# A hybrid SSD, GLA, cross-attention and SwiGLU block on one core: the Strassen-Winograd sums of three weights made by accumulating DRAM transfers instead of GpSimd

## The chip, the cores and the metric
The kernel runs on one core of a Trainium2 chip, as one launch. The metric is the device time of one execution, in microseconds (us), as the median of several runs. Five engines work beside one another, each through its own queue, in order: PE (TensorE: matmuls, with PEld, its weight loads), DVE (VectorE), ACT (ScalarE), POOL (GpSimd) and SP (SyncE, which here only issues DMAs). 16 DMA engines move the data of all queues.

## The reference, cut to what matters
One decoder block over a sequence of 1024 rows with D = 1024: an SSD branch and a GLA branch on one projection `w_in`, merged through gates, then cross-attention to 256 rows of memory, then SwiGLU with d_ff = 2816. All in float32. The three products that the change touches are those with `w_o`, `w_xq` and `w_ffn_out`:

```python
    merged = jax.nn.sigmoid(g_ssd) * (y_ssd @ w_up_ssd) + jax.nn.sigmoid(g_gla) * (y_gla @ w_up_gla)
    return merged @ w_o
    ...
    q = (n @ w_xq).reshape(Bsz, S, XATTN_HEADS, XATTN_HEAD_DIM)
    ...
    g, u = jnp.split(n @ w_ffn_in, 2, axis=-1)
    return (jax.nn.silu(g) * u) @ w_ffn_out
    ...
        h = h + hybrid_mixer(rmsnorm(h, norm_mix[i]), ...)
        h = h + mem_cross_attention(rmsnorm(h, norm_xattn[i]), ...)
        h = h + swiglu(rmsnorm(h, norm_ffn[i]), w_ffn_in[i], w_ffn_out[i])
    return rmsnorm(h, norm_final)
```

## The kernel before
**Products.** Every operand in float32 is split into a high part (`hi`, a rounding copy on ACT) and a low part (`lo`, a subtraction on DVE), and each product is three matmuls of 128x512: hi x lo, hi x hi, lo x hi. Where it pays, a product is a Strassen-Winograd product over 2x2 blocks: seven block products named `B11`, `B21`, `B22`, `T1` to `T4` in place of eight. Each needs sums of blocks of the weight (S1 to S4) and of the activations, and after it the results are added up (`evac` and `fevac`). `T1h`/`T1l` are the split halves of an activation sum, `whi`/`wlo` those of a streamed weight, `ws` those of w_o and w_xq, `fs` those of w_ffn_out.

**Stages, in us from the span's start.** Keys, values and the input up to 160; the units of z (160 to 240) and of xBC with the convolution (240 to 390), each a 1 MB load `raw` of w_in; the remaining units with SSD and GLA woven in to 800; the two up-projections, dense, to 980; w_o (class `Wide`) to 1040 and w_xq to 1100; attention to 1205; w_xo, dense, to 1281; the first SwiGLU product to 1705, in 11 pairs of a gate unit and an up unit, 38.8 us a pair; the down-projection to 1905; the closing norm to 1940. In a unit the sums of the weight are made on the fly from `raw`: `sa<-raw`, `sa<-sa,raw`, `raw<-raw` and `raw<-raw,sa`, on POOL or DVE. A helper `either` takes the engine that by a running count (`Meter`, a time per instruction and element) is free first. In such counts the calls on POOL are included, DMAs too.

**The sums of the three other weights.** They don't fit that pattern, since `Wide` and the down-projection load S1 to S4 from DRAM (`wos_d`, `xqs_d`, `down_d`). `presum(part, key)` (from line 1401) writes them. Per block of 128 rows it loads the four quadrants (1 MB) from the weight, makes the sums with four TENSOR_TENSORs on POOL (one addition and three subtractions) and stores each with an SP DMA of 256 KB. 8 blocks are of w_o and w_xq, 11 of w_ffn_out: 19 blocks, 76 sums. It runs in three parts: `early` (blocks 0 to 7, w_o and w_xq) in the up-projections, 800 to 980 us, with the buffer `pre` in a slot of the pool "m"; `late` (blocks 8 to 12) in attention and w_xo, with `pre` in a slot of the pool "op"; `last_sums` (blocks 13 to 18) in SwiGLU, over four `ga` tiles. The slots of "op" are handed on: when `late` ends, the slot that `pre` had is used by the split `B21l` of SwiGLU's activations, whose residual rows are `o` and `ga`. Around line 1700 the loop over w_xo takes two steps of `late` for each product.

**Order.** A tile scheduler orders the instructions by data dependences and priorities; `pinned` keeps an instruction at the place where it is written. `run(main, (side, rate))` draws `rate` steps of a side generator for each step of the main one. Each queue then runs in that order.

## Time and profile before
| | us |
|---|---|
| median of 3 runs | 1945.46 (1941.2 to 1947.19) |
| profiled execution | 1941.48 |
| its span | 1939.8 |
| PE busy | 1900.3 (98%) |
| DVE busy | 1391.4 (72%) |
| ACT busy | 879.8 (45%) |
| POOL busy | 611.7 (32%) |
| mean granted clock of TensorE | 0.995 of full speed |

The span is the time from the first to the last instruction of the profiled execution. A share of busy time is a mean over stages with different limits; which wait ends last in a stage tells what a change there can be worth. The rows below are in the form of the profile: start, duration, engine, line, operation, out<-in, and in brackets the idle time before the instruction with what ended it.

### The profile page before, as it was taken

How to read it: one execution, taken by the hardware profiler on the slowest of the kernel's cores; microseconds unless marked ns; L12 is line 12 of the kernel's file. 1: busy time of each engine (PE TensorE's matmuls, PEld its weight loads, DVE VectorE, ACT ScalarE, POOL GpSimd, SP SyncE). 2: the span in 40 equal slices, each digit the busy share in tenths (PEclk: the TensorE clock that was granted, in tenths of full speed). 3: DMA queues.
4: the chain of work that ended last, by engine and by line, in shares of the span. 5: the costliest groups of instructions: out<-in, count | busy, mean ns of one | idle time of the engine just before them, and what ended most of it. 6: DMA issues, size and time to landing. Idle time of an engine off the chain costs nothing.

```text
span 1939.8 us, 26274 instructions
## 1 busy us (share of the span) xinstructions
PE 1900.3 (98%) x9680; PEld 1599.7 (82%) x9680; DVE 1391.4 (72%) x1926; ACT 879.8 (45%) x1521; POOL 611.7 (32%) x455
## 2 busy tenths in 40 slices
...
GB/s 343 144 94 102 131 300 115 147 163 183 184 161 121 208 169 125 330 356 273 229 174 202 177 66 47 261 137 114 137 163 152 130 150 150 50 298 246 156 222 124
DMA packets 245365, 341.06 MB, mean 176 GB/s; under 512 B 17370, under 2 KB 148676, under 8 KB 245236
## 3 DMA queue, kind: packets, MB, share of 16 engines
q1 hardware_dynamic: 243508, 333.09, 50.7%
...
## 4 chain that ended last, share of the span: by engine, by line
PE 76%; DVE 9%; DMA 7%; POOL 3%; issue 3%; ACT 2%; SPq 0%; POOLq 0%; DVEq 0%; ACTq 0%
PE acc L51 60%; PE bank L51 14%; DVE cv L73 2%; POOL pre L73 2%; DVE wlo L73 2%; PE bank L55 2%; DMA pre<-in_w_xq_dram 1%; DMA pre<-in_w_ffn_out_dram 1%; DVE o L73 1%; DMA zr<-sz_d 1%; DVE hs L73 1%; POOL sa L73 1%; DMA down_d<-pre 1%; DMA xqs_d<-pre 1%; DMA wr<-wos_d 0%
## 5 line engine op out<-in xcount | busy, mean ns | idle before, releaser
L73 DVE TENSOR_TENSOR wlo<-raw,whi 128x512 fp32r<-128x512 f32 x272 | 245.8, 912 | 96.8 <-ACT whi L229 94.6
L229 ACT ACTIVATE whi<-raw 128x512 fp32r<-128x512 f32 x272 | 169.4, 628 | 237.4 <-PE acc L51 191.3
L51 PE MATMUL acc<-hl,wd 128*128 128x512 f32 x1152 | 263.8, 390 | 1.7 <-ACT wd L229 1.3
L51 PEld LDWEIGHTS acc<-hl,wd 128*128 128x128 f32 x1152 | 215.5, 188 | 48.3 <-ACT wd L229 2.5
L73 DVE TENSOR_TENSOR o<-acc,o 128x512 f32<-128x512 f32 (+1 forms) x256 | 172.3, 674 | 86.9 <-PE acc L51 77.4
L51 PE MATMUL acc<-fs 128*128 128x512 f32 (+1 forms) x792 | 155.7, 355 | 0.1
L51 PEld LDWEIGHTS acc<-fs 128*128 128x128 f32 x792 | 130.7, 189 | 20.8 <-issue 0.5
L73 DVE TENSOR_TENSOR fs<-fr,fs 128x1024 fp32r<-128x1024 f32 (+1 forms) x84 | 98.9, 1217 | 37.5 <-ACT fs L229 37.4
L229 ACT ACTIVATE fs<-fr 128x1024 fp32r<-128x1024 f32 (+1 forms) x84 | 79.0, 982 | 96.0 <-PE acc L51 30.7
L73 POOL TENSOR_TENSOR raw<-raw,sa 128x512 f32<-128x512 f32 x44 | 57.4, 1305 | 202.3 <-DVE wlo L73 202.3
L73 POOL TENSOR_TENSOR sa<-pre 128x512 f32<-128x512 f32 x13 | 19.3, 1485 | 290.0 <-DMA pre<-in_w_o_dram 103.1
L229 ACT ACTIVATE whi<-sa 128x512 fp32r<-128x512 f32 x96 | 59.6, 626 | 94.8 <-PE acc L51 89.2
L73 POOL TENSOR_TENSOR sa<-raw 128x512 f32<-128x512 f32 x43 | 68.4, 1590 | 106.5 <-DMA raw<-in_w_in_dram 77.0
L73 DVE TENSOR_TENSOR wlo<-sa,whi 128x512 fp32r<-128x512 f32 x96 | 82.2, 856 | 14.2 <-ACT whi L229 13.3
L51 PE MATMUL acc<-ws 128*128 128x512 f32 x384 | 89.1, 390 | 1.7 <-DVE ws L73 1.7
L51 PEld LDWEIGHTS acc<-ws 128*128 128x128 f32 x384 | 71.8, 188 | 17.2 <-DVE ws L73 2.2
L51 PE MATMUL acc<-B11h,whi 128*128 128x512 f32 x192 | 75.9, 395 | 2.5 <-ACT whi L229 2.5
L51 PE MATMUL acc<-T4h,whi 128*128 128x512 f32 x192 | 76.2, 397 | 2.0 <-DVE o L73 2.0
L51 PE MATMUL acc<-T1h,wlo 128*128 128x512 f32 x192 | 76.0, 396 | 1.7 <-DVE wlo L73 1.7
L51 PE MATMUL acc<-B11h,wlo 128*128 128x512 f32 x192 | 76.0, 396 | 1.5 <-DVE wlo L73 1.5
L51 PE MATMUL acc<-B22h,wlo 128*128 128x512 f32 x192 | 75.8, 395 | 1.5 <-DVE wlo L73 1.4
L51 PE MATMUL acc<-T1h,whi 128*128 128x512 f32 x192 | 77.2, 402 | 0.0
...
## 6 DMA issues: line engine op xcount, KB each, us to landing
raw<-in_w_in_dram SPq DMA_DIRECT2D x26, 1024.0 KB, 5.9
raw<-in_w_ffn_in_dram SPq DMA_DIRECT2D x22, 1024.0 KB, 9.3
...
fr<-act_d SPq DMA_DIRECT2D x35, 512.0 KB, 6.1
fr<-down_d SPq DMA_DIRECT2D x20, 512.0 KB, 4.7
...
csb<-cs_d SPq DMA_DIRECT2D x15, 512.0 KB, 4.4
fr<-in_w_ffn_out_dram SPq DMA_DIRECT2D x15, 512.0 KB, 3.8
```

Source lines behind the costliest of these rows:

```text
L51: return s.e.matmul(o, x, y, **kw)
L55: return s.e.transpose(o, x, i)
L73: return f(*a, **kw)
L229: ACT.activation(hi, src, AF.Copy)
```

## The change
`presum` and its three parts are gone. In place of them `weight_sums` makes the four sums with DMAs from DRAM to DRAM, issued on POOL's queue: a plain copy of a quadrant of the weight into the place of a sum, or a transfer that adds to what lies there (`accum_op=ALU.add`). For w_o and w_xq it runs in the units of z and xBC (`wsums`, rate 0.36; 24 DMAs: per weight four copies of 1 MB and four accumulations, each cut in two of 0.5 MB), for w_ffn_out in the pairs of SwiGLU (`last_sums`, groups of 3, 3, 3 and 2 blocks; 32 DMAs of 0.75 or 0.5 MB). Nothing is summed from 390 us to SwiGLU. An accumulating transfer can only add, so the second block row of the weight is taken with the other sign: all four sums then are sums with plus. The signs are made good elsewhere: by operands in the other order in the sums of the activations, by a split with `neg` (scale -1 in ACT's copy, SCALAR_TENSOR_TENSOR for the low half) for the right operand of `T2`, and by sub for add, or a scale of -1, in the evacuations.

```diff
+    def split(src, hi, lo, e=None, neg=False, pin=lambda x: x):
+        if neg:
+            pin(ACT.activation(hi, src, AF.Copy, scale=-1.0))
+            pin(DVE.scalar_tensor_tensor(lo, src, -1.0, hi, ALU.mult, ALU.subtract))
...
+    def weight_sums(todo):
+        jobs = []
+        for A, d, n, k0 in todo:
+            put = lambda m, d=d, n=n, k0=k0, kn=A.shape[2]: (
+                d[(m * n + k0) * P:(m * n + k0 + kn) * P].rearrange("(k p) c -> p k c", p=P))
+            q = {(i, j): A[j][:, :, half(i)] for i in range(2) for j in range(2)}
+            jobs.append([(put(0), q[1, 0], 0), (put(2), q[0, 0], 0), (put(3), q[0, 1], 0), (put(0), q[1, 1], 1),
+                         (put(2), q[1, 0], 1), (put(1), put(0), 0), (put(1), q[0, 0], 1), (put(3), put(1), 1)])
+        for step in zip(*jobs):
+            for o, a, more in step:
+                kn = o.shape[1]
+                for c in (slice(0, kn // 2), slice(kn // 2, kn)) if more and kn > 3 else (slice(0, kn),):
+                    if more:
+                        pinned(POOL.dma_start(o[:, c], a[:, c], accum_op=ALU.add))
+                    else:
+                        pinned(POOL.dma_start(o, a))
+                    yield
...
-    run(singles(zu, B, xu[:1]), (prep, 1.0))
+    run(singles(zu, B, xu[:1]), (prep, 1.0), (wsums, 0.36))
...
+    drain(wsums)
...
-                    DVE.scalar_tensor_tensor(o, p, s.scale, o, ALU.mult, ALU.add)
+                    DVE.scalar_tensor_tensor(o, p, -s.scale if i else s.scale, o, ALU.mult, ALU.add)
                 elif first:
-                    ACT.activation(o, p, AF.Copy)
+                    ACT.activation(o, p, AF.Copy, scale=-1.0 if i else 1.0)
+                elif name == "T3":
+                    sub(DVE, o, o, p)
...
-    early = presum(slice(0, 8), "m")
...
-    late = presum(slice(8, 13), "op")
...
-    last_sums = presum(slice(13, None), "ga")
+    w_down = t["w_ffn_out"].rearrange("(k j p) c -> j p k c", j=2, p=P)
+    last_sums = chain(weight_sums([(w_down[:, :, k:min(k + 3, KP)], down_d, KP, k)]) for k in range(0, KP, 3))
...
-        run(group([gate], B, () if last else gu[u + 1][:1]), (last_sums, 0.33))
+        run(group([gate], B, () if last else gu[u + 1][:1]), (last_sums, 0.4))
...
-            if n in (2, 5):
+            if n == 2:
                 next(last_sums, None)
```

The instructions of the changed program: PE 9171 matmuls as before and in nearly the same order, ACT 1465 as before, DVE 1947 for 1924 (10 more `raw<-raw,sa`, 10 more `o<-o,ssum`, 3 others), POOL 417 for 460 (76 sums gone, 23 moved to DVE, 56 DMAs come), SP 687 for 800.

**POOL in the units of z.** `raw` is the weight unit, `sa` its sums; the numbers tell buffers apart. Before:

```order
L73 TENSOR_TENSOR raw_1941<-raw_1941,sa_1988 128x4x128 [waits DVE_49,Pool_49]
L73 MEMSET keep_2053 128x1 [waits Pool_49]
L73 MEMSET keep_2053 128x1 x7
L73 TENSOR_TENSOR sa_2200<-raw_2170 128x512 [waits DMAHW0_49]
L73 TENSOR_TENSOR sa_2202<-sa_2200,raw_2170 128x512 [waits Pool_49]
L73 TENSOR_TENSOR raw_2170<-raw_2170 128x4x128
L73 TENSOR_TENSOR raw_2170<-raw_2170,sa_2202 128x4x128 [waits DVE_49,Pool_49]
L73 TENSOR_TENSOR sa_2354<-raw_2326 128x512 [waits DMAHW1_49]
L73 TENSOR_TENSOR sa_2356<-sa_2354,raw_2326 128x512 [waits Pool_49]
L73 TENSOR_TENSOR raw_2326<-raw_2326 128x4x128
L73 COPY ebm_1938<-gy0_2096 128x8 [waits DVE_49]
```

After:

```order
L73 DMA wos_d_82<-in_w_o_dram 128x4x512
L73 TENSOR_TENSOR sa_2202<-raw_2172 128x512 [waits DMAHW0_49]
L73 TENSOR_TENSOR sa_2204<-sa_2202,raw_2172 128x512 [waits Pool_49]
L73 TENSOR_TENSOR raw_2172<-raw_2172 128x4x128
L73 DMA wos_d_82<-in_w_o_dram 128x4x512
L73 DMA xqs_d_83<-in_w_xq_dram 128x4x512
L73 DMA wos_d_82<-in_w_o_dram 128x4x512
L73 TENSOR_TENSOR sa_2359<-raw_2330 128x512 [waits DMAHW1_49,DVE_49,Pool_49]
L73 TENSOR_TENSOR sa_2361<-sa_2359,raw_2330 128x512 [waits DVE_49,Pool_49]
L73 TENSOR_TENSOR raw_2330<-raw_2330 128x4x128
L73 DMA xqs_d_83<-in_w_xq_dram 128x4x512
```

Four copies of 1 MB each, one ahead of the sums of one unit and three behind them in a row, now stand on POOL's queue around these sums; none of the four waits for another transfer.

**POOL in the middle of SwiGLU.** `o` is the gated result and `ssum` a part of SiLU; `ga` the sums of w_ffn_out. Before:

```order
L73 TENSOR_TENSOR raw_12065<-raw_12065,sa_12249 128x4x128 [waits DVE_49]
L73 TENSOR_TENSOR sa_12551<-raw_12369 128x512 [waits DMAHW2_49]
L73 TENSOR_TENSOR sa_12553<-sa_12551,raw_12369 128x512 [waits Pool_49]
L73 TENSOR_TENSOR raw_12369<-raw_12369 128x4x128
L73 TENSOR_TENSOR o_12228<-o_12228,ssum_9967 128x512 [waits DMAHW5_49,Activation_49]
L73 TENSOR_TENSOR o_12228<-o_12228,ssum_9967 128x512 [waits Activation_49] x2
L73 TENSOR_TENSOR ga_12073<-ga_12073,ga_12071 128x512 [waits DMAHW1_49]
L73 TENSOR_TENSOR raw_12219<-raw_12219,sa_12397 128x4x128 [waits DVE_49]
```

After:

```order
L73 TENSOR_TENSOR o_12680<-o_12680,ssum_9910 128x512 [waits DMAHW0_49,Activation_49]
L73 DMA down_d_81<-down_d_81 128x3x512 [waits DMASW2_49]
L73 DMA down_d_81<-in_w_ffn_out_dram 128x3x512 [waits DMASW6_49,DMASW5_49]
L73 TENSOR_TENSOR o_12680<-o_12680,ssum_9910 128x512 [waits Activation_49]
L73 TENSOR_TENSOR raw_12671<-raw_12671,sa_12847 128x4x128 [waits DVE_49]
L73 DMA down_d_81<-down_d_81 128x3x512 [waits DMASW6_49,DMASW4_49]
L73 TENSOR_TENSOR sa_13137<-raw_12963 128x512 [waits DMAHW0_49]
```

The sum on `ga` is gone, one `o<-o,ssum` is on DVE, and three transfers came in: a copy of the second sum's start, an accumulation onto it that waits for that copy (DMASW6), and one that waits for the accumulation; two instructions of POOL lie between the last two.

**DVE at the entry to SwiGLU.** `B21l<-o,B21h` is the low half of an activation block, `ga<-acc,ga` the evacuation of w_xo onto the residual. Before:

```order
L73 TENSOR_TENSOR ssum_9967<-ssum_9967,sq_11127 128x512 [waits DVE_49,Activation_49]
L73 TENSOR_TENSOR B21l_11306<-o_10626,B21h_11305 128x512 [waits DMAHW4_49,DMAHW3_49,DMAHW6_49,DMAHW0_49,Pool_49]
L73 TENSOR_TENSOR B21l_11306<-o_10626,B21h_11305 128x512
L73 TENSOR_TENSOR o_10626<-o_10626,o_10624 128x512 [waits DVE_49] x2
L73 SCALAR_TENSOR_TENSOR ga_11056<-acc_11141,ga_11056 128x512 [waits DMAHW1_49,PE_49]
L73 TENSOR_TENSOR ssum_9967<-ssum_9967,sq_11169 128x512 [waits Activation_49]
L73 TENSOR_TENSOR B21l_11306<-o_10627,B21h_11305 128x512 [waits Activation_49]
```

After:

```order
L73 TENSOR_TENSOR ssum_9910<-ssum_9910,sq_10984 128x512 [waits Activation_49]
L73 TENSOR_TENSOR B21l_11198<-o_10569,B21h_11197 128x512 [waits Activation_49]
L73 TENSOR_TENSOR o_10569<-o_10569,o_10567 128x512 [waits DVE_49]
L73 SCALAR_TENSOR_TENSOR ga_10919<-acc_10993,ga_10919 128x512 [waits DMAHW3_49,DMAHW2_49,PE_49]
L73 TENSOR_TENSOR o_10568<-o_10570,o_10568 128x512 [waits Activation_49]
L73 TENSOR_TENSOR o_10568<-o_10570,o_10568 128x512
L73 TENSOR_TENSOR ssum_9910<-ssum_9910,sq_11021 128x512 [waits Activation_49]
L73 SCALAR_TENSOR_TENSOR ga_10954<-acc_11033,ga_10954 128x512 [waits DMAHW6_49,DMAHW4_49,PE_49]
```

`B21l` waited for four DMA semaphores and POOL, the stores and sums of `pre`, with two `ga` evacuations behind it; now it waits for ACT, and the evacuations follow one another with single pieces of `B21l` between them.

## Rows read from the trace of the kernel before
**Rows 1.** The page's first part: engine, busy us (share of span), instructions.

```profile
PE 1900.3 (98%) x9680; PEld 1599.7 (82%) x9680; DVE 1391.4 (72%) x1926; ACT 879.8 (45%) x1521; POOL 611.7 (32%) x455
```

**Rows 2.** Stretches: length; busy PE, PEld, DVE, ACT, POOL; clock; DMA share; GB/s.

```profile
160.00:240.00 80.00, 78.43 (x346) 62.05 (x345) 58.32 (x73) 44.20 (x71) 31.93 (x35) 1.00 0.37 124
240.00:300.00 60.00, 58.96 (x258) 47.69 (x257) 48.23 (x53) 34.83 (x48) 21.20 (x17) 1.00 0.74 264
300.00:390.00 90.00, 88.98 (x413) 72.50 (x413) 79.02 (x82) 50.97 (x77) 31.14 (x18) 1.00 0.38 133
1250.00:1300.00 50.00, 44.11 (x176) 35.12 (x176) 36.46 (x54) 23.47 (x42) 11.49 (x8) 0.90 0.52 177
1302.00:1705.00 403.00, 402.83 (x1784) 333.16 (x1783) 332.92 (x383) 142.47 (x241) 233.52 (x152) 1.00 0.40 133
```

**Rows 3.** Rows of time, entry to SwiGLU.

```profile
1275.81 1.29 DVE L73 TENSOR_TENSOR B21l<-o,B21h 128x512 fp32r<-128x512 f32 x2 [10.25 <-DMA down_d<-pre]
...
1278.94 0.72 ACT L1697 ACTIVATE o<-ga,cols 128x512 f32<-128x512 f32 x1 [14.79 <-DVE ga L73]
...
1281.28 0.50 PE L51 MATMUL acc<-B11h,whi 128*128 128x512 f32 x1 [2.51 <-ACT whi L229]
...
1283.49 0.79 PE L51 MATMUL acc<-B11h,wlo 128*128 128x512 f32 x1 [1.49 <-DVE wlo L73]
...
1293.22 0.50 PE L51 MATMUL acc<-B21h,whi 128*128 128x512 f32 x1 [0.33 <-ACT whi L229]
...
1295.53 0.50 PE L51 MATMUL acc<-T1h,wlo 128*128 128x512 f32 x1 [1.57 <-DVE wlo L73]
```

**Rows 4.** Rows of time, entry to w_o.

```profile
989.51 1.06 ACT L1245 ACTIVATE ws<-wr 128x1024 fp32r<-128x1024 f32 x1 [4.78 <-DMA wr<-wos_d]
...
1000.48 0.73 PE L51 MATMUL acc<-ws 128*128 128x512 f32 x2 [1.74 <-DVE ws L73]
```

**Rows 5.** Groups of POOL: count, busy us, mean ns, idle before.

```profile
L73 POOL TENSOR_TENSOR pre<-pre 128x512 f32<-128x512 f32 x26 | 41.2, 1605 | 0.0
...
L73 POOL TENSOR_TENSOR ga<-ga 128x512 f32<-128x512 f32 x24 | 40.4, 1686 | 4.0 <-DMA ga<-in_w_ffn_out_dram 3.4
...
L73 POOL TENSOR_TENSOR pre<-sa,pre 128x512 f32<-128x512 f32 x13 | 19.7, 1514 | 1.0
...
L73 POOL TENSOR_TENSOR sa<-pre 128x512 f32<-128x512 f32 x13 | 19.3, 1485 | 290.0 <-DMA pre<-in_w_o_dram 103.1 <-DMA pre<-in_w_ffn_out_dram 100.6 <-DMA h_d<-ga 49.3
```

**Rows 6.** Rows of time of two pairs in SwiGLU.

```profile
1414.93 1.29 POOL L73 TENSOR_TENSOR sa<-raw 128x512 f32<-128x512 f32 x1 [3.50 <-DMA raw<-in_w_ffn_in_dram]
...
1421.50 0.39 PE L51 MATMUL acc<-B11h,whi 128*128 128x512 f32 x1
...
1430.41 0.68 DVE L73 TENSOR_TENSOR wlo<-raw,whi 128x512 fp32r<-128x512 f32 x1
...
1431.17 1.29 POOL L73 TENSOR_TENSOR raw<-raw,sa 128x512 f32<-128x512 f32 x1 [1.23 <-DVE wlo L73]
...
1432.49 0.63 ACT L229 ACTIVATE whi<-raw 128x512 fp32r<-128x512 f32 x1 [0.34 <-POOL raw L73]
...
1437.82 0.39 PE L51 MATMUL acc<-B22h,whi 128*128 128x512 f32 x1
```

**Rows 7.** The page's DMA queue (packets, MB, share); issues (count, KB, us landing).

```profile
q1 hardware_dynamic: 243508, 333.09, 50.7%
...
raw<-in_w_ffn_in_dram SPq DMA_DIRECT2D x22, 1024.0 KB, 9.3
...
fr<-down_d SPq DMA_DIRECT2D x20, 512.0 KB, 4.7
```

**Rows 8.** DMA issues from 160 to 390 us.

```profile
raw<-in_w_in_dram SPq DMA_DIRECT2D x12, 1024.0 KB, 9.7
```

**Rows 9.** Waits from 245 to 300 us: in total, times, longest.

```profile
POOL sa L73 <- DMA raw<-in_w_in_dram: 14.4, 2, 7.6
...
PE acc L51 <- DVE wlo L73: 0.9, 1, 0.9
```

More of the change, by code (lines that the diff above doesn't have):

```diff
@@ L225, in spread @@
             pin(PE.matmul(p[:, c * P:(c + 1) * P], r[:, c:c + 1].to_broadcast([P, P]), ident, start=True, stop=True))
-    def split(src, hi, lo, e=None):
-        ACT.activation(hi, src, AF.Copy)
-        sub(e or DVE, lo, src, hi)
+    def split(src, hi, lo, e=None, neg=False, pin=lambda x: x):
[3 more added lines that the diff above has]
+        else:
+            pin(ACT.activation(hi, src, AF.Copy))
+            pin(sub(e or DVE, lo, src, hi))
     def wring():
@@ L869, in block_kernel @@
     prep = chain([ssd_prep(), gla_prep()])
-    run(singles(zu, B, xu[:1]), (prep, 1.0))
+    wsums = weight_sums([(t[w].rearrange("(j k p) c -> j p k c", j=2, p=P), d, 4, 0) for w, d in (("w_o", wos_d), ("w_xq", xqs_d))])
+    run(singles(zu, B, xu[:1]), (prep, 1.0), (wsums, 0.36))
     drain(prep)
@@ L1026, in block_kernel @@
     for n, u in enumerate(XU):
-        run(group([xu[n]], B, (xu + ru)[n + 1:n + 2]), (pend, 1.0))
+        run(group([xu[n]], B, (xu + ru)[n + 1:n + 2]), (pend, 1.0), (wsums, 0.36))
         drain(pend)
@@ L1241, in prep @@
                     if name in s.COMB:
-                        o, a, b = (s.quad(*ij)[:, c] for ij in s.COMB[name])
-                        sub(s.two(o), o, a, b)
-                    for src, o in ((s.raw[m][:, c], x[0]), (s.quad(*s.RIGHT[name])[:, c], x[1])):
-                        pin(ACT.activation(o[:, 0], src, AF.Copy))
-                        pin(sub(DVE, o[:, 1], src, o[:, 0]))
+                        f, *q = s.COMB[name]
+                        o, a, b = (s.quad(*ij)[:, c] for ij in q)
+                        f(s.two(o), o, a, b)
+                    split(s.raw[m][:, c], x[0][:, 0], x[0][:, 1], pin=pin)
+                    split(s.quad(*s.RIGHT[name])[:, c], x[1][:, 0], x[1][:, 1], neg=name == "T2", pin=pin)
                 s.ops.append(x)
@@ L1332, in hl, with into @@
         return slots_[k]
-    def into(slots_, k, j, src, e=None):
+    def into(slots_, k, j, src, e=None, neg=False):
         x = hl(slots_, k)
-        split(src, x[:, 0, half(j)], x[:, 1, half(j)], e)
+        split(src, x[:, 0, half(j)], x[:, 1, half(j)], e, neg)
     def dense(no, ins, post, pre=lambda o, j: None, js=JS, left=left):
@@ L1504, in residual @@
         return post
-    xq = Wide(t["w_xq"], xqs_d, lambda i, j, u, p: into(i_q, 4 * i + u, j, p), ("m", "m", "aux", "aux", "m", "aux", "aux"), ("m", "m", "aux"))
+    xq = Wide(t["w_xq"], xqs_d, lambda i, j, u, p: into(i_q, 4 * i + u, j, p, neg=(i, j) == (1, 0)), ("m", "m", "aux", "aux", "m", "aux", "aux"), ("m", "m", "aux"))
     def put_xq(o, j, q, g):
@@ L1515, in waiting @@
             yield
-    early = presum(slice(0, 8), "m")
-    run(dense(0, i_ys, post_ys, lambda o, j: gate(gs_d, o, j)), (fetch_gated(yg_d, sr_d, i_yg), 1.0), (waiting(early, 2), 1.2))
-    run(dense(1, i_yg, post_yg, lambda o, j: (gate(gg_d, o, j), quad(ysg_d, o * P, 0, j))), (early, 1.5),
-        (wide_side(wo, 8, 4, pinned), 1.0))
-    drain(early)
+    run(dense(0, i_ys, post_ys, lambda o, j: gate(gs_d, o, j)), (fetch_gated(yg_d, sr_d, i_yg), 1.0))
+    run(dense(1, i_yg, post_yg, lambda o, j: (gate(gg_d, o, j), quad(ysg_d, o * P, 0, j))), (wide_side(wo, 8, 4, pinned), 1.0))
     run(wo.steps(), (wide_side(xq, 7, 2), 1.0))
@@ L1700, in block_kernel @@
     for n, _ in enumerate(dense(0, i_xo, residual(h2_d, u_xo_stats, "norm_ffn", put_xo), quad_of(h1_d), js=(1, 0), left=left_xo)):
-        for _ in range(2):
-            next(late, None)
         if n >= 8:
```

63 lines of the change are left out of this document (13 added, 50 removed).

## The prediction
> **What bounds the kernel now.** I read the page's first part, then the table of stretches, then the rows of time around the places that the change touches. The page says PE is busy 98% of the span, DVE 72% and POOL 32% [rows 1]; POOL work that disappears is therefore worth something only where somebody on PE's path waits for it. The reader should look in the table of stretches for those where PE is not full [rows 2]. In SwiGLU's main part (1302 to 1705 us) PE is busy 402.83 of 403.00 us, so nothing is to be won there. In 160 to 390 us it lacks 1.57, 1.04 and 1.02 us. The stretch 1250 to 1300 is the hole: PE 44.11 of 50.00 us, granted clock 0.90.
>
> The rows of time there show why [rows 3]. The 13th weight-sum block (in the buffer `pre`) is still being stored while the cross-attention's last projection ends. DVE's `B21l` split takes over the slot of `pre` and waits 10.25 us for the DMA `down_d<-pre`; on DVE's queue the residual evacuations `ga` stand behind it, so ACT's `o<-ga` is 14.79 us late, and PE then lacks `whi`, `wlo` four times: 2.51 + 1.49 + 0.33 + 1.57 = 5.90 us. The granted clock of 0.90 says that PE also ran a part of this stretch at 1.2 GHz, the lower of its levels, so more is lost than the gaps. Sized by rate: the full stretch ran 1784 matmuls in 403.00 us, 0.2259 us each; 1250 to 1300 ran 176, worth 39.8 us, so 10.2 us are lost there.
>
> The second place is the entry to w_o [rows 4]: ACT waits 4.78 us for `wr<-wos_d`, PE 1.74 us for `ws`. SP issues those loads behind the loads and stores of the sums of w_xq.
>
> **What goes.** 76 TENSOR_TENSORs on POOL: the groups of `pre` and `ga` sum to 41.2 + 40.4 + 19.7 + 19.3 = 120.6 us [rows 5]. On SP 113 DMAs go (13 loads of `pre`, 24 of `ga`, 76 stores). PE keeps its 9171 matmuls. Of this only two things were on the path. At the entry to SwiGLU the slot is no longer held: in the changed order `B21l` waits for ACT alone, its first pieces are spread between the `ga` evacuations, and no such sum runs from 980 us to 1281 us. Late next is the first pair's own DVE work (the 1.57 us gap before `T1h,wlo` was on DVE), which stays, as DVE still makes that pair's sums. So of 10.2 us I take 8.5 as won, with bounds 5 (the evacuation chain after the last matmul takes part of it back) and 10.2. At w_o all sums have been stored since about 390 us, so the 1.74 us go; I take 1.7.
>
> **What changes sign costs nothing.** One more scaling by -1 is a parameter of ACT's copy; 14 TENSOR_TENSORs become SCALAR_TENSOR_TENSORs of the same shape, and additions become subtractions. The work stays on the same engine with the same count, beside a PE that DVE (332.92 of 403.00 us busy) keeps supplied [rows 2]. Bound: 14 times a fraction of 1 us on DVE, on nobody's path. 23 sums move from POOL to DVE, two per pair of SwiGLU (`raw<-raw,sa` and `o<-o,ssum`), 1.29 us each on POOL; DVE's `wlo` of the same shape takes 0.68 us [rows 6]. Ten pairs by twice 1.29 us is at most 26 us on a DVE that had 70 us idle in that stretch, so I cost it at nothing; without that cover a late `wlo` would hold PE by the same 1.29 us, twice a pair.
>
> **What comes: 56 transfers from DRAM to DRAM on POOL's queue**, 24 between 160 and 390 us (8 MB copied, 8 MB accumulated) and 32 in SwiGLU (11 MB and 11 MB). No row shows such a transfer or its issue on POOL, so I bound each by loads from DRAM [rows 7, 8]: 512 KB of `down_d` land in 4.7 us, 1024 KB of w_ffn_in in 9.3 us, 1024 KB of w_in in 9.7 us between 160 and 390.
>
> *Engines of the DMA.* Queue q1 moved 333.09 MB in 50.7% of 1939.8 us, 2.95 us of all 16 engines for a MB [rows 7]. 16 MB cost 47 us if a DRAM to DRAM MB costs what a load costs, 94 us at double. Over the 230 us from 160 to 390 that adds 0.20 to 0.41 to shares of 0.37, 0.74 and 0.38 [rows 2]: 240 to 300 comes to between 0.94 and 1.15, the only stretch that can run full. There POOL already waited 14.4 us in two waits for `raw<-in_w_in`, and PE felt 0.9 us of it [rows 9]. At a share of 1.15 the stretch has 0.15 x 60 = 9 us too much work, some of which falls into its neighbours. Bounds 0 and 9, I take 2: PE lost almost nothing of 14.4 us of waiting, and a unit is loaded ahead. In SwiGLU 22 MB come (65 to 130 us) and 12 MB of the old loads and stores go (six blocks of 1 MB in and 1 MB out, 35 us): 0.40 becomes 0.47 to 0.64, not full.
>
> *POOL held by its own transfers.* An accumulating transfer has to wait for the one that wrote the same rows; the wait stands in POOL's order, and everything behind it waits too. In each group of eight steps the last three form such a chain. In most places a product or more lies between them. Five times in SwiGLU the next stands next to it or two instructions on, as in the order shown: copy, accumulate, `o<-o,ssum`, `raw<-raw,sa`, accumulate. A 0.75 MB transfer lies between 4.7 and 9.3 us; I take 7. Behind it: POOL's `raw<-raw,sa` at 1431.17, 1.29 us, then ACT's `whi` at 1432.49, whose product begins at 1437.82 [rows 6]. From 1431.17 that is 6.65 us, less the sum (1.29), `whi` (0.63) and `wlo` (0.68): 4.05 us of slack. The stage sums have 1421.50 (the `B11h` that first uses the load) less 1414.93 = 6.57 us. A hold of 7 us after which the sum stands immediately would cost PE 3 us, but the hold begins when POOL is otherwise idle, as POOL's idle entries show (1.23 and 3.50 us). Bounds 0 and 5 x 5.3 (9.3 - 4.05) = 26 us, I take 1. In the z units, four in 78.43 us of PE work, 19.6 us each, three copies of 1 MB stand between the sums of two units. At 9.7 us a copy, each held until the one before it is done, that is 29.1 us, 9.5 more than a unit; if issuing holds nothing, 0. I take 0.5, nearest to the latter, as none of the three waits for a transfer in the order.
>
> The Trainium skill ("Perfetto Trace Analysis", DMA Instruction - SWDGE (GPSIMD)) says that an engine may begin to consume descriptors before the generation ends, particularly if more are generated than fit in the buffer; by it POOL would stand in the triple copy while the data moves, the 0.5 would become 9.5 and the sum 1947.8 us. No row here shows it; it speaks for rival one, whose sum goes by the loads above.
>
> **The sum.** Profiled execution 1941.48 us (span 1939.8). -8.5 - 1.7 + 2 + 0.5 + 1 = -6.7, so 1934.8. The median of the runs shown stands 3.98 us above the profiled execution: 1938.8 us.
>
> **Rivals.** *One: POOL and the DMA engines become the bound, slower.* If an accumulating transfer takes 9 us or more, its five holds in SwiGLU cost about 4 each (20 us less what their spacing hides, say 12), and the full stretch 240 to 300 costs 9 with the lower clock behind it (about 2). -10.2 + 12 + 9 + 2 + 1 = +14, 1959 us on the median. For it: slack of only 4.05 us, share 0.74 already. Against it: the scheduler leaves a product or more between most. It decides where 0.75 MB takes longer than 4.05 us of slack plus the idle entry ahead of the sum (1.23 to 3.50 us), so from about 7.5 us on.
> *Two: given back, no change.* The gap at the entry goes, but the first pairs of z, xBC and SwiGLU get late by 2 to 4 us in all three places: -10.2 + 10 = 0, 1945 us. For it: the bounds of the costs, 9, 9.5 and 26, are wide compared with the gain.
> *Three: the change does not free the entry.* PE's 2.51 us gap waits for `whi`, and ACT has its own queue of splits for the first pair there. If the backlog is the chain of evacuations and not the slot, only 1.74 + 2 go, and the costs of 3.5 cancel them: 1945 us. Against it: the 10.25 us wait names the store.
> *Four: all of it is won* and the transfers stay hidden: -11.9, 1933.5 us.
>
> **How the numbers follow.** Forecast (1933 to 1939.6) with rival four together 0.50; what of the forecast falls short, with rivals two and three, 0.24; rival one 0.26. About 0.3% (5.8 us) is what a measurement of this kernel can tell from no change: faster is below 1939.6, slower above 1951.3. The range goes from 1929 (all won, on a run below the median) to 1957 (nearly rival one).
>
> **What would show it.** Right: no wait of `B21l` for a DMA, PE 47 us or more of 1250 to 1300 at clock 0.95 or more, no wait for `wr<-wos_d` over 2 us, PE above 402 of the stretch in SwiGLU. Wrong: PE gaps behind POOL's `raw` or `sa` in SwiGLU, POOL waits for its own transfers of more than 4 us with PE waiting after them, PE below 57 of 60 us in 240 to 300, or `raw<-in_w_in` landing in more than 12 us.

## The result and the profile after
The changed kernel takes 1948.87 us (median of 15 runs, 1946.56 to 1953.25), the kernel before on the same chip 1943.60 us (15 runs, 1940.86 to 1947.19): a ratio of 1.0027, interval [1.0019, 1.0035]. The forecast was 1938.8 us, faster. The time lies in the range but on the other side: slower by 0.27%, which is inside the 0.3% that the prediction called no change (the interval reaches 0.35%), and nearest to the 1945 us of rivals two ("given back") and three. The profiled execution took 1951.16 us (span 1949.5), 9.7 us more than that of before; of these, 4.4 us are the distance of the two profiled executions from their medians (2.3 above, 2.1 below). All sums below are made between the profiled executions, so they explain 9.7 and not 5.3.

The first part of the page after answers to [rows 1]:

```profile
PE 1901.7 (98%) x9680; PEld 1598.3 (82%) x9680; DVE 1352.9 (69%) x1949; ACT 880.5 (45%) x1521; POOL 509.4 (26%) x412
```

POOL has lost 102 us of work, PE's share is the same. The stretches after, with the columns of [rows 2]:

```profile
160.00:240.00 80.00, 77.58 (x340) 61.35 (x340) 56.85 (x77) 43.81 (x71) 32.18 (x39) 1.00 0.67 208
240.00:300.00 60.00, 53.11 (x216) 41.48 (x215) 33.60 (x40) 28.71 (x40) 22.32 (x21) 0.94 0.98 289
300.00:390.00 90.00, 81.92 (x348) 65.47 (x349) 73.91 (x76) 40.77 (x56) 36.04 (x25) 0.96 0.69 187
1000.00:1030.00 30.00, 30.00 (x134) 24.86 (x133) 27.48 (x29) 11.85 (x12) 0.00 (x0) 1.00 0.48 175
1250.00:1300.00 50.00, 50.00 (x223) 41.40 (x221) 34.03 (x51) 23.60 (x40) 0.00 (x0) 1.00 0.32 110
1302.00:1705.00 403.00, 402.93 (x1792) 333.32 (x1792) 323.85 (x411) 141.72 (x242) 192.02 (x138) 1.00 0.56 153
```

The hole at the entry to SwiGLU is closed: PE is busy 50.00 of 50.00 us at clock 1.00, where it was 44.11 at 0.90. SwiGLU is as full as before (402.93 for 402.83). The new holes are in xBC: 53.11 of 60 us at clock 0.94, and 81.92 of 90 at 0.96, where before had 58.96 and 88.98 at 1.00.

Windows at fixed times mix different work once one kernel lags. The clearer measure is worked out from both traces: take the start of the same matmul in each and subtract. The median difference, after minus before, in us, by the time of before at which that matmul ran:

```
at            200   250   265   290   310   350   365   400   950  1100  1225  1320  1680  1880
after        -0.6   1.0   9.7  11.1  12.5  12.8  18.5  22.4  23.4  21.3  20.7   9.5   9.3   9.3
```

So z and xBC lose 23.0 us (-0.6 to 22.4), 1.0 more goes until 950, the entry to w_o gives back 2.1, attention and the start of w_xo to 1225 another 0.6, the entry to SwiGLU 11.2, and SwiGLU 0.2. Of the 23.0, 8.7 go in one step at 250 to 265 and 9.4 in another at 350 to 390; the other 4.9 are spread over smaller losses that are not split here.

PE's two long gaps there, from the rows of time of after, stand at the same two places (granted clock below 1 in both stretches: part of what follows each gap runs at 1.2 GHz, so a step is larger than its gap):

```profile
265.29 0.79 PE L51 MATMUL acc<-B22h,whi 128*128 128x512 f32 x1 [5.82 <-ACT whi L233]
...
382.89 0.80 PE L51 MATMUL acc<-T2h,whi 128*128 128x512 f32 x1 [5.39 <-ACT whi L233]
```

What ACT waited for is on POOL's queue. Rows of time of POOL around the first gap, after, and one of ACT (in the brackets: idle time ahead, and what ended it; `issue` is a wait for nothing that the profile shows):

```profile
235.74 1.17 POOL L73 DMA_DIRECT2D wos_d<-in_w_o_dram  x1
244.46 1.14 POOL L73 DMA_DIRECT2D xqs_d<-in_w_xq_dram  x1 [7.55 <-issue]
...
252.67 1.16 POOL L73 DMA_DIRECT2D xqs_d<-in_w_xq_dram  x1 [5.37 <-issue]
...
262.14 1.14 POOL L73 DMA_DIRECT2D wos_d<-in_w_o_dram  x1 [7.30 <-issue]
262.88 1.70 POOL L73 TENSOR_TENSOR raw<-raw,sa 128x512 f32<-128x512 f32 x1
...
264.61 0.63 ACT L233 ACTIVATE whi<-raw 128x512 fp32r<-128x512 f32 x1 [12.85 <-POOL raw L73]
```

Three issues, one after the other, each stood 5.4 to 7.6 us at the head of POOL's queue, and behind them stood the sum `raw<-raw,sa`, which ACT, and then PE, waited for. The waits of 160 to 420 us (in total, times, longest) show that this is the rule there:

```profile
POOL xqs_d L73 <- issue: 39.9, 9, 8.1
...
POOL wos_d L73 <- issue: 23.0, 5, 7.3
ACT whi L233 <- POOL raw L73: 20.4, 5, 12.8
...
ACT whi L233 <- POOL sa L73: 16.5, 3, 12.4
```

62.9 us in 14 waits, and none of them stands in the order: there a transfer waits for a semaphore only where it follows another on the same rows. Four of the 14 lie in z (13.4 us together; the longest, 6.5, ended at 186 us) and cost PE next to nothing (77.58 of 80 us, before 78.43). What they wait for shows where it is missing: in SwiGLU two copies of 0.75 MB go out 2.0 us apart, from POOL's rows of time after:

```profile
1546.87 0.78 POOL L73 DMA_DIRECT2D down_d<-in_w_ffn_out_dram  x1
...
1548.89 0.78 POOL L73 DMA_DIRECT2D down_d<-in_w_ffn_out_dram  x1
```

whereas in z and xBC, with copies of 1 MB and accumulations of 0.5 MB, 14 of the 24 transfers stood waiting in this way, eight of them for 4.9 to 8.1 us. That looks like a limit on what is under way from POOL's queue, not on the data. The table of the DMA queues, 160 to 400 us of after (packets, MB, share of 16 engines; under it issues, KB each, us to landing), adds the second suspect:

```profile
q1 hardware_dynamic: 19872, 28.61, 34.8%
q0 software_dynamic: 6528, 16.78, 32.4%
...
raw<-in_w_in_dram SPq DMA_DIRECT2D x11, 1024.0 KB, 10.3
```

POOL's transfers (q0) take 32.4% of 240 us for 16.78 MB, 4.6 us of all engines a MB, the loads and stores of q1 2.9. The 4.6 is a mean of two prices. From 160 to 212 us POOL's transfers are plain copies (six), from 213 to 297 us they are accumulations (eight); the same table of after for these two stretches:

```profile
q0 software_dynamic: 1632, 6.29, 37.1%
...
q0 software_dynamic: 2148, 4.17, 32.6%
```

37.1% of 52 us for 6.29 MB is 3.1 us a MB, about the price of a load; 32.6% of 84 us for 4.17 MB is 6.6 us, twice as much.

### The profile page after: what moved, and what is told of

It is laid out like the page before. It is cut to its first block, busy times and chain, and to the rows that moved or that the text cites. A ratio compares the mean times of both kernels' runs of the same rounds, so it can differ in the third digit from the quotient of the medians.

```text
span 1949.5 us, 26093 instructions
## 1 busy us (share of the span) xinstructions
PE 1901.7 (98%) x9680; PEld 1598.3 (82%) x9680; DVE 1352.9 (69%) x1949; ACT 880.5 (45%) x1521; POOL 509.4 (26%) x412
## 3 DMA queue, kind: packets, MB, share of 16 engines
q10 hardware_dynamic: 1728, 6.29, 0.8%
## 4 chain that ended last, share of the span: by engine, by line
PE 84%; DVE 7%; issue 4%; POOL 2%; DMA 2%; ACT 1%; SPq 0%; POOLq 0%; DVEq 0%; ACTq 0%
PE acc L51 68%; PE bank L51 15%; PE bank L55 2%; DVE cv L73 2%; DVE wlo L73 2%; DVE hs L73 1%; DVE o L73 1%; DMA hl<-ys_d 0%; DMA down_d<-in_w_ffn_out_dram 0%; POOL ssum L73 0%; POOL raw L73 0%; DVE gx L73 0%; DMA raw<-in_w_ffn_in_dram 0%; DVE gy L73 0%; ACT cv L778 0%
## 5 line engine op out<-in xcount | busy, mean ns | idle before, releaser
L73 DVE TENSOR_TENSOR wlo<-raw,whi 128x512 fp32r<-128x512 f32 x272 | 237.6, 880 | 114.2 <-ACT whi L233 111.8
L73 DVE TENSOR_TENSOR o<-acc,o 128x512 f32<-128x512 f32 x244 | 167.2, 685 | 89.6 <-PE acc L51 85.8
L73 DVE TENSOR_TENSOR fs<-fr,fs 128x1024 fp32r<-128x1024 f32 (+1 forms) x78 | 93.0, 1226 | 36.7 <-ACT fs L233 36.5
L73 POOL TENSOR_TENSOR ssum<-ssum,sq 128x512 f32<-128x512 f32 (+1 forms) x17 | 29.5, 1733 | 322.4 <-ACT sq L519 308.8
L73 POOL TENSOR_TENSOR sa<-raw 128x512 f32<-128x512 f32 x42 | 62.7, 1494 | 134.8 <-DMA raw<-in_w_in_dram 65.9
L73 DVE TENSOR_TENSOR wlo<-sa,whi 128x512 fp32r<-128x512 f32 x96 | 75.5, 787 | 23.9 <-ACT whi L233 23.0
L73 POOL TENSOR_TENSOR raw<-raw,sa 128x512 f32<-128x512 f32 x34 | 47.8, 1406 | 138.0 <-DVE wlo L73 138.0
L51 PE MATMUL acc<-B22h,whi 128*128 128x512 f32 x192 | 76.9, 400 | 6.1 <-ACT whi L233 5.8
L51 PE MATMUL acc<-T2h,whi 128*128 128x512 f32 x192 | 76.8, 400 | 5.7 <-ACT whi L233 5.7
L51 PE MATMUL acc<-T3h,wlo 128*128 128x512 f32 x192 | 75.4, 393 | 1.5 <-DVE wlo L73 1.5
```

Of the source, the lines that this page charges most:

```text
L51: return s.e.matmul(o, x, y, **kw)
L73: return f(*a, **kw)
```

## Experiments
**Theory**: the room for the descriptors of POOL's transfers is too small for those of z and xBC; POOL's queue stands until room is there, the sums behind it come late ("holds"). **Rival**: the crowd on the DMA engines; the transfers slow the loads of the units. Where the runs are compared by the shift of the same matmul, it is this table (us against before, at times of before; read as the row above; three kernels that do nothing new in z and xBC, e7, e9 and e12, stand between -0.9 and 0.1 at 400 us, so a microsecond is not to be read):

```
at                   200   400   950  1100  1225  1320  1680  1880
after               -0.6  22.4  23.4  21.3  20.7   9.5   9.3   9.3
e1_ring2048         -0.8  11.1  12.4  10.4   9.7  -1.5  -2.1  -2.1
e5_skip              1.0   7.3   7.8   5.8   5.1  -6.1  -6.7  -6.7
e10_place_ring       0.4   5.7   6.5   4.5   3.8  -7.4  -7.9  -7.9
e11_place            0.2  48.7  47.8  45.8  45.2  33.9  34.0  34.0
e2_gla               0.1  -1.5  20.9  18.9  18.2   7.0   7.0   7.0
e4_copies              -   2.3  24.3  22.3  21.7  10.4  10.5  10.5
e6_gla_ring          0.3  -1.2  38.8  36.8  36.1  24.9  24.5  24.5
e8_ssd_gla_ring      0.1   0.9  15.2  13.2  12.5   1.3   0.8   0.8
e7_no_late          -0.3  -0.8   0.5   0.6   0.0 -11.2  -8.8  -8.1
e9_ffn_only         -0.3  -0.9  -1.9  -1.4  -2.1 -13.3 -13.0 -13.0
e12_ffn_ring         0.9   0.1   1.0   1.0   0.4 -10.8 -11.3 -11.3
```

### The room doubled
Only the argument for the room of those descriptors changes; the order of all instructions stays.

```diff
-    nc = _bacc.Bacc("TRN2", target_bir_lowering=False, num_devices=1, dynamic_dma_scratch_size=1024)
+    nc = _bacc.Bacc("TRN2", target_bir_lowering=False, num_devices=1, dynamic_dma_scratch_size=2048)
```

> The changed kernel with twice the descriptor space for GpSimd's transfers (2048 bytes for 1024), nothing else. Theory A: between 160 and 400 us GpSimd stands for 62.9 us before its own transfers because the space takes one at a time; then more than half of these waits go and the time falls by 8 to 16 us, to 1933 to 1941 us. Theory B: the waits are for data, or the DMA engines are full (share 0.98 from 240 to 300) whatever stands in GpSimd's order: within 3 us of 1948.9.

Measured: 1942.03 us, ratio 0.9993 [0.9981, 1.0004], between the two expectations. The waits of 160 to 420 us, this kernel:

```profile
POOL wos_d L73 <- issue: 0.3, 1, 0.3
```

62.9 us have become 0.3: it was the room. But of the 23.0 us only 11.1 come back; 11.9 are still lost by 400 us, 9.5 of them in one step at 250 to 265. Rows of time of this kernel there, and behind them the same sum in before:

```profile
248.77 0.44 SPq L299 DMA_DIRECT2D raw<-in_w_in_dram  x1
...
268.05 1.27 POOL L73 TENSOR_TENSOR sa<-raw 128x512 f32<-128x512 f32 x1 [15.64 <-DMA raw<-in_w_in_dram]
...
268.76 0.80 PE L51 MATMUL acc<-B11h,whi 128*128 128x512 f32 x1 [7.30 <-ACT whi L233]
```

```profile
247.97 0.42 SPq L295 DMA_DIRECT2D raw<-in_w_in_dram  x1
...
257.71 1.41 POOL L73 TENSOR_TENSOR sa<-raw 128x512 f32<-128x512 f32 x1 [7.57 <-DMA raw<-in_w_in_dram]
```

The load of the first xBC unit is used 19.3 us after its issue (248.77 to 268.05), 9.7 before (247.97 to 257.71); PE, which had not felt the 7.57, stands 7.30 us. In this run POOL issues five accumulations of 0.5 MB between 235.6 and 250.4 us. Two of them have landed before the load is issued (at 243.4 and 246.8 us); three are under way with it and land at 257.9, 262.7 and 266.1 us. The time from issue to landing of that load, in after and in this run:

```profile
raw<-in_w_in_dram SPq DMA_DIRECT2D x1, 1024.0 KB, 13.3
...
raw<-in_w_in_dram SPq DMA_DIRECT2D x1, 1024.0 KB, 19.2
```

In after the waits for room let the accumulations out one at a time (beside the load mainly that of 252.67 us, landed at 261.8), and the load landed at 264.0 us, 6 us before POOL, held once more, came to it (270.17 us); the sum `raw<-raw,sa` that PE missed there belongs to the unit before, and what it needs from DVE, `wlo`, was done at 252.7. So both causes are real, and at the first place they don't add: 8.7 us with holds, 9.5 without them, from the load alone. No run has holds at that place without the data; that they make the step in after is read from these rows. The second step, 9.4 us at 350 to 390, is the room's alone: here that stretch loses 1.0 (10.1 to 11.1).

### No transfers beside the first xBC unit
The room of 2048, and the units of xBC give out transfers from the second on.

```diff
-        run(group([xu[n]], B, (xu + ru)[n + 1:n + 2]), (pend, 1.0), (wsums, 0.36))
+        run(group([xu[n]], B, (xu + ru)[n + 1:n + 2]), (pend, 1.0), (wsums, 0.42 if n else 0.0))
```

> As e1 (twice the descriptor space), and no transfer is given out in the first xBC unit (rate 0.42 in the later ones for 0.36 in all). Theory: what e1 still lost (9.5 us at 240 to 270 us) is the load of the first xBC unit, which shared the DMA engines with five transfers issued from 235 to 250 us and landed after 19 us instead of 10; with two of them there it lands in 14 us or less and the time is 1931 to 1937 us. Rival: 16 MB more of traffic between 160 and 400 us cost that much wherever they stand there: 1939 to 1944 us.

Measured: 1934.32 us, 0.9955 [0.9941, 0.9968], 0.38 points of a per cent below the room alone; the loss to 400 us falls from 11.9 to 6.3. POOL's rows of time of this kernel:

```profile
237.34 1.17 POOL L73 DMA_DIRECT2D wos_d<-in_w_o_dram  x1
238.09 1.60 POOL L73 DMA_DIRECT2D xqs_d<-in_w_xq_dram  x1
...
248.48 1.14 POOL L73 DMA_DIRECT2D xqs_d<-in_w_xq_dram  x1
...
263.92 1.47 POOL L73 TENSOR_TENSOR sa<-raw 128x512 f32<-128x512 f32 x1 [11.76 <-DMA raw<-in_w_in_dram]
```

Three transfers instead of five precede the sum, and two of them have landed before the load is issued at 250.53 us (at 245.1 and 248.6 us); one is beside it, and the sum starts 13.4 us after the issue. With no accumulation beside it the load landed after 9.7 us (before), with one at a time after 13.3 (after and e5), with three after 19.2 (e1): that is the crowd.

### The room small again where the placing is good
e10 gives out five transfers in the first two units of z and the rest from the third xBC unit on, denser (0.7), with the room of 2048. e11 is the same with 1024.

```diff
-    run(singles(zu, B, xu[:1]), (prep, 1.0), (wsums, 0.36))
+    run(singles(zu, B, xu[:1]), (prep, 1.0), (itertools.islice(wsums, 5), 0.36))
...
-        run(group([xu[n]], B, (xu + ru)[n + 1:n + 2]), (pend, 1.0), (wsums, 0.36))
+        run(group([xu[n]], B, (xu + ru)[n + 1:n + 2]), (pend, 1.0), (wsums, 0.7 if n > 1 else 0.0))
```

> As e5 (twice the descriptor space), with no transfer from the third unit of z to the second of xBC: five in the first two units of z, the others from the third unit of xBC on at rate 0.7. Theory: e5's rest (6.7 us, from 225 to 300 us) are transfers beside the loads of that stretch; without them 1927 to 1931 us. Rival: 19 transfers in the last four units of xBC crowd the DMA engines there (share 0.38 before) and cost 4 us or more: 1932 to 1940 us.

> As e10 with the descriptor space of the changed kernel (1024 bytes). If the holds cost by themselves, away from the crowded stretch: GpSimd stands 4 to 9 us before each transfer that follows another, its sums in the last four units of xBC are late: 8 us or more slower than e10. If only the crowded stretch counts: within 3 us of e10.

Measured: e10 1933.49 us, 0.9947 [0.9933, 0.9960], inside its rival's 1932 to 1940; e11 1977.45 us, 1.0181 [1.0167, 1.0195]. Nothing differs but the room, and it is worth 43 us (shift at 400 us: 5.7 and 48.7). The waits of 160 to 420 us, e10 and then e11:

```profile
POOL xqs_d L74 <- issue: 6.0, 2, 5.7
...
POOL wos_d L74 <- issue: 3.0, 2, 2.3
PE acc L52 <- ACT whi L234: 2.1, 3, 1.4
```

```profile
POOL wos_d L74 <- issue: 53.5, 11, 7.6
POOL xqs_d L74 <- issue: 46.2, 10, 7.4
...
PE acc L52 <- ACT whi L234: 38.1, 5, 17.1
```

The denser the transfers stand, the more a small room costs. Of the 5.3 us that e10 still loses to 400 us, 4.9 go at 320 to 390 us of before, where its transfers now are, at a DMA share of 0.87 for 300 to 390 (before 0.38 [rows 2]).

### The early sums somewhere else
e2 puts the transfers of w_o into GLA and those of w_xq into the second up-projection, none into z and xBC; room 1024. (POOL has nothing ahead of those of w_xq and issues them from 805 us on, in the first up-projection.) `w_o_sums` and `w_xq_sums` are `weight_sums` of one weight each.

```diff
-    run(singles(zu, B, xu[:1]), (prep, 1.0), (wsums, 0.36))
+    run(singles(zu, B, xu[:1]), (prep, 1.0))
...
-    run(singles(gs[2:] + gg[:3], B, gg[3:]), (gla, 8 * 5 / 30), prio=PRIO)
+    run(singles(gs[2:] + gg[:3], B, gg[3:]), (gla, 8 * 5 / 30), (w_o_sums, 0.36), prio=PRIO)
...
-    run(dense(1, i_yg, post_yg, lambda o, j: (gate(gg_d, o, j), quad(ysg_d, o * P, 0, j))), (wide_side(wo, 8, 4, pinned), 1.0))
+    run(dense(1, i_yg, post_yg, lambda o, j: (gate(gg_d, o, j), quad(ysg_d, o * P, 0, j))), (wide_side(wo, 8, 4, pinned), 1.0), (w_xq_sums, 0.8))
+    drain(w_xq_sums)
```

> The sums of w_o are moved to the GLA stage (640 to 800 us) and those of w_xq into the second up-projection (890 to 980 us), same transfers, rest of the change as it is. If the loss is only where they stood (160 to 400 us, about 22 us by the shift of equal matmuls) and the gains at w_o and SwiGLU are real (2 and 11 us): 1928 to 1934 us. If the transfers cost as much wherever they stand: 1945 or more.

Measured: 1951.00 us, 1.0040 [1.0028, 1.0051]. z and xBC are whole again (-1.5 at 400): the transfers there, and nothing else of the change, made the 23 us. But GLA and the up-projection lose about as much. POOL works in GLA on small tiles `ss` that ACT, and then PE, wait for, and a transfer stands ahead of them. POOL's rows of time of e2:

```profile
664.77 1.17 POOL L73 DMA_DIRECT2D wos_d<-in_w_o_dram  x1 [6.62 <-issue]
665.54 1.49 POOL L73 TENSOR_TENSOR ss<-ss,mhalf 128x4 f32<-128x4 f32 x1
...
706.90 1.14 POOL L73 DMA_DIRECT2D wos_d<-in_w_o_dram  x1 [6.80 <-DMA wos_d<-wos_d]
707.64 1.48 POOL L73 TENSOR_TENSOR ss<-ss,mhalf 128x4 f32<-128x4 f32 x1
```

PE's gaps behind them are 4.72 and 4.18 us. The first hold is the room's; the second is the one that I had foreseen for SwiGLU, a transfer that waits for the one before it on the same rows.

e3 adds to e2 24 times eight small POOL MEMSETs at the old places of the transfers, as holds without data; e4 adds 24 plain copies, 16 MB in all, from DRAM to DRAM on ACT's queue there, as data without holds. Both are work that the reference doesn't ask for.

```diff
+            for _ in range(8):
+                pinned(nc.gpsimd.memset(hold, 0.0))
```

```diff
+                pinned(ACT.dma_start(e[0:HALF, :], w[0:HALF, half(n // 2 % 2)]))
```

> As e2, and in the units of z and xBC 24 holds of GpSimd (eight MEMSETs of 128x256 each, about 4 us) at the places where the transfers stood, with no transfer there. Theory A (GpSimd held, its sums late): 8 to 20 us slower than e2. Theory B (full DMA engines): within 3 us of e2.

> As e2, and in the units of z and xBC 24 plain copies from DRAM to DRAM (16 MB in all) on ACT's queue, which GpSimd does not wait for. Theory A: within 4 us of e2. Theory B: 8 to 20 us slower than e2, with loads of w_in landing in 12 us or more.

Measured: e3 1950.05 us, 1.0036 [1.0024, 1.0048], no slower than e2. It decides nothing: the MEMSETs (about 0.37 us each, 13.6 us in the longest clump) stand where POOL has time, and ACT's `whi` waits for POOL come to 3.9 us from 160 to 420, where after has 36.9; the holds were not rebuilt. Why the order came out so is not shown. e4: 1955.70 us, 1.0062 [1.0040, 1.0083], between its two expectations; z and xBC lose 3.8 us more than in e2 (2.3 for -1.5 at 400), with the load of the first xBC unit used 14.4 us after its issue (248.05 to 262.46). So as many MB without POOL cost 4 us: the crowd again, though smaller than in e1. It is the milder test: its transfers are all plain copies, and around that load they are four of 0.5 MB (235.0 to 252.3 us), where e1 has five accumulations, at twice the price a MB.

e6 is e2 with the room of 2048 (the edit of e1). e8 moves the transfers of e6 earlier, those of w_o to SSD and those of w_xq to GLA:

```diff
-        run(singles(ru + qk + gs[:2], B, gs[2:3]), (ssd, 80 / 70), prio=PRIO)
+        run(singles(ru + qk + gs[:2], B, gs[2:3]), (ssd, 80 / 70), (w_o_sums, 0.18), prio=PRIO)
...
-    run(singles(gs[2:] + gg[:3], B, gg[3:]), (gla, 8 * 5 / 30), (w_o_sums, 0.36), prio=PRIO)
+    run(singles(gs[2:] + gg[:3], B, gg[3:]), (gla, 8 * 5 / 30), (w_xq_sums, 0.36), prio=PRIO)
```

> As e2 (sums of w_o in the GLA stage, of w_xq behind them), with twice the descriptor space. Theory: e2 lost 21 us at 640 to 830 us because GpSimd, held before its transfers, gave the normalisation of GLA (`ss`) late to ACT and PE; without holds the time is 1929 to 1937 us. Rival: the DMA engines are shared with the loads of GLA and of the up-projection, no matter how GpSimd stands: 1944 us or more.

> Twice the descriptor space, the sums of w_o in the SSD stage (rate 0.18), those of w_xq in the GLA stage (0.36), the rest of the change as it is. If holds and the crowded 240 to 270 us were the whole loss: before less 2 (w_o) less 11 (SwiGLU) less 1 to 3 us, 1926 to 1931 us. If the transfers cost 2 to 5 us in each of the two stages: 1933 to 1939 us.

Measured: e6 1965.05 us, 1.0114 [1.0100, 1.0128], inside the rival's "1944 us or more", but that it would be slower than e2 neither foresaw. More room made it slower: eight transfers of w_xq now go out between 795 and 822 us, at the start of the up-projection (two in e2), and what that needs from DRAM comes late: ACT waits 15.02 us for `hl`, in e2 3.4 at most. Rows of time of e6:

```profile
820.53 1.15 ACT L1396 ACTIVATE hl<-hl,cols 128x1024 fp32r<-128x1024 f32 x1 [15.02 <-DMA hl<-ys_d]
...
828.04 2.07 PE L51 MATMUL acc<-hl,wd 128*128 128x512 f32 x4 [17.87 <-ACT wd L233]
```

With the small room, waits for room of 8.7 to 9.3 us had spread these transfers out. e8: 1943.44 us, 1.0004 [0.9995, 1.0013], also not what was expected. The hold in GLA that no room cures is still there, from its rows of time:

```profile
708.11 1.14 POOL L73 DMA_DIRECT2D xqs_d<-in_w_xq_dram  x1 [8.09 <-DMA xqs_d<-xqs_d]
708.87 1.46 POOL L73 TENSOR_TENSOR ss<-ss,mhalf 128x4 f32<-128x4 f32 x1
...
710.89 0.69 PE L55 MATMUL bank<-ident,o 128*128 128x128 f32 x2 [3.96 <-ACT o L1145]
```

### The gains by themselves
e7 is the kernel before, without any transfer that accumulates: the sums that were made by POOL in the attention phase (`late`) are made in SwiGLU with the others.

```diff
-    late = presum(slice(8, 13), "op")
+    late = iter(())
...
-    last_sums = presum(slice(13, None), "ga")
+    last_sums = presum(slice(8, None), "ga")
...
-        run(group([gate], B, () if last else gu[u + 1][:1]), (last_sums, 0.33))
+        run(group([gate], B, () if last else gu[u + 1][:1]), (last_sums, 0.5))
```

e9 is the changed kernel with only w_ffn_out summed by transfers: the sums of w_o and w_xq go back to POOL in the up-projections, by a `presum` with plus, as the signs of the change want it; the diff shows its sums. e12 is e9 with the room of 2048.

```diff
-    run(singles(zu, B, xu[:1]), (prep, 1.0), (wsums, 0.36))
+    run(singles(zu, B, xu[:1]), (prep, 1.0))
...
+    early = presum()
...
+                for n, (o, x, y) in enumerate(((s1_, a(1, 0), a(1, 1)), (a(1, 1), s1_, a(0, 0)),
+                                               (a(1, 0), a(0, 0), a(1, 0)), (a(0, 1), a(0, 1), a(1, 1)))):
+                    add(POOL, o, x, y)
```

> The kernel before with one thing changed: the five blocks of w_ffn_out that were summed in attention and w_xo (`late`) are summed in SwiGLU with the other six, on GpSimd as they were, at rate 0.5 for 0.33. If the 10.2 us at the entry to SwiGLU come from the slot of `pre`, they go with no transfer that accumulates: 1929 to 1935 us. If they come from the chain of evacuations: 1939 us or more. If 20 more sums make GpSimd late in SwiGLU: PE below 400 of the 403 us there.

> One part of the change alone: w_ffn_out by accumulating transfers in SwiGLU, with the descriptor space of the changed kernel; w_o and w_xq summed on GpSimd in the up-projections as in the kernel before (with the signs of the change). If the loss is all between 160 and 400 us and the transfers in SwiGLU cost nothing: 11 us less than before, 1930 to 1933 us, the gap of 1.74 us at w_o is back. If GpSimd's holds in SwiGLU cost something once the rest is right: 1936 us or more.

> As e9 with twice the descriptor space. In SwiGLU GpSimd stood 21.6 us in six waits for room and 21.3 us in four for data before its transfers, and PE was full there all the same. If those holds cost nothing: within 2 us of e9 (1928.8), with the waits for room gone. If they cost something unseen, 3 us or more faster; if more transfers side by side slow the loads of w_ffn_in, 3 us or more slower.

Measured: e7 1933.42 us, 0.9953 [0.9938, 0.9969]; e9 1928.81 us, 0.9929 [0.9916, 0.9941], which beats both kernels; e12 1929.47 us, 0.9936 [0.9923, 0.9950], the same as e9. The entry to SwiGLU gives 11.2 us in all three (shift from 1225 to 1320), and in e7 without any transfer: the gain there comes from not holding the slot, whoever makes the sums. e9 is 4.6 us faster than e7 by the medians (1933.42 less 1928.81). From 1320 to 1880 e7, with five more blocks to sum in SwiGLU, falls back by 3.1 us (-11.2 to -8.1), e9 by 0.3: these 2.8 us are what the transfers of w_ffn_out are worth beyond the slot. The rest, 2.1 by the shift, is there by 1225 us, where neither run sums w_ffn_out by transfers, and stays unexplained. The stretch 1302 to 1705 of e7 and of e9, columns as in [rows 2] (in e12 PE is busy 403.00 us of it):

```profile
1302.00:1705.00 403.00, 401.93 (x1766) 330.28 (x1765) 337.82 (x376) 141.97 (x236) 250.41 (x165) 1.00 0.46 158
```

```profile
1302.00:1705.00 403.00, 402.43 (x1775) 332.81 (x1774) 321.98 (x394) 143.24 (x237) 193.44 (x138) 1.00 0.58 165
```

And the waits of POOL's transfers in that stretch, e9 and then e12:

```profile
POOL down_d L73 <- issue: 21.6, 6, 5.3
POOL down_d L73 <- DMA down_d<-in_w_ffn_out_dram: 16.9, 3, 7.2
```

```profile
POOL down_d L73 <- DMA down_d<-in_w_ffn_out_dram: 16.8, 3, 7.1
```

The waits for room go with the larger room, the waits for data stay, and neither changes the time: in SwiGLU POOL may stand 5 to 7 us, PE does not feel it.

## Why the prediction was wrong
**The failed step** is the pair of terms for z and xBC: 2 for the crowd and 0.5 for the triple copy, 2.5 taken, 23.0 measured between the profiled executions. In the changed kernel the hold is the larger part: the two steps that end behind held sums are 18.1 of the 23.0. Two things went wrong in that step.

*The hold.* I looked in the order for what a transfer waits for, and called an issue without a semaphore almost free: "I take 0.5, nearest to the latter, as none of the three waits for a transfer in the order". The wait that came stands in no order; it is for room (62.9 us in 14 waits, 0.3 with the room doubled, e1). I had priced it at one place only, the triple copy in z, where a whole unit lay behind it and two waits (6.5 us, and 6.6 that the profile puts down to `wlo`) indeed cost next to nothing (PE 77.58 of 80, before 78.43 [rows 2]). In xBC three such waits follow one another ahead of one sum, and later two more. The bound of 9.5 belonged to every bunch of transfers with a sum behind it, not to one. The Trainium skill ("Perfetto Trace Analysis", DMA Instruction — SWDGE (GPSIMD)) says that a DMA engine may begin to consume descriptors before their generation ends, particularly if more are generated than fit in the buffer. The trace agrees that there is such a limit (62.9 us of waits, 0.3 with the room doubled); that POOL's queue stands meanwhile is what I had worked out from it, and the rows show it. The sum by it, 1947.8 us, came near to the 1948.87 measured by luck: I had applied it at another place, and the gain at the entry was larger than taken.

*The crowd.* I had the share of 240 to 300 right (0.94 to 1.15 foreseen, 0.98 measured) and priced it by the average: 2, at most 9. e1 shows that it hits one load: 19.3 us instead of 9.7, and 9.5 us lost in a step, because PE waited for that load alone and three transfers stood beside it. Of POOL's 15.64 us of waiting PE felt 7.30 there, so the cover was some 8.3 us (an estimate), of which before used 7.57: that PE had felt 0.9 of 14.4 us [rows 9] said that the slack was almost used up, not that there was more. I had also taken one price for all 16 MB, one to two times a load's: copies cost one, and the accumulations beside that load two. A rule about the sharing stands in the Trainium skill ("DMA: Bandwidth & Descriptors", Issuing engines are not separate DMA queues): transfers started by ACT, SP or POOL run on the same 16 engines and interleave there. e4 agrees, with 3.8 us lost to copies from ACT's queue.

**What held.** *Entry to SwiGLU*: 8.5 taken, bounds 5 and 10.2, measured 11.2, a microsecond beyond the upper bound; nothing was taken back by the chain of evacuations (PE 50.00 of 50.00 at clock 1.00), and e7 shows that the held slot was the cause, against rival three (the sums and stores of `late` leave attention with it; they are not told apart from the slot). *w_o*: 1.7 taken, 2.1 measured; the matmul that had waited at 1000.48 us [rows 4] stands near 1022 in after, and PE is busy 30.00 of 30.00 us at 1000 to 1030. *Signs and the sums moved to DVE*: nothing foreseen, none found: DVE has 323.85 us in SwiGLU (332.92 before [rows 2]), and e9, which has all the signs, loses nothing up to 1225. *SwiGLU's holds*: five of some 7 us foreseen; four came (17.1 us in three, 4.3 in one), the longest 7.0, and seven waits for room (21.4) that I had not foreseen; 1 us taken, a gain of 0.2 measured. e12 shows that they are covered. The DMA share is 0.56 (0.47 to 0.64 foreseen).

**The sum as measured**: 23.0 in z and xBC, 1.0 to 950, -2.1 at w_o, -0.6 to 1225, -11.2 at the entry, -0.2 in SwiGLU make 9.9, from a shift of -0.6 at 200: 9.3 at 1880, of the 9.7 between the executions. With 2.5 in place of the 23.0 it would have come to -10.6, where -6.7 was forecast: the gain at the entry was larger and the cost in SwiGLU smaller than taken.

**The rivals.** Two ("given back") has the result: gains of the size foreseen, eaten by late units; it named z and xBC among its places. One (POOL and the DMA engines become the bound) had the mechanisms, a hold of POOL and a full stretch of 240 to 300, but put the hold in SwiGLU, where there is cover, where holds of up to 7.2 us (e9) cost nothing. Two of the signs that the prediction named for being wrong came: PE below 57 of 60 us at 240 to 300 (53.11), and a load of w_in landing in more than 12 us (13.3 for the first xBC unit, though 10.3 in the median).

**What stays open**: the 6.3 and 5.3 us that e5 and e10 still lose in xBC are not split further (several gaps of 1.2 to 1.4 us behind ACT and DVE, a share of the DMA engines of 0.98 for e5 at 240 to 300 and of 0.87 for e10 at 300 to 390); nor are the roughly 5 us that e8 loses little by little in SSD, where the waits for `csb<-cs_d` grow from 17.5 to 22.9 us.
